# Half-block products in the output product of two feed-forward layers

## The chip, the cores and the metric

The kernel runs on one core of a Trainium2 chip. The metric is the time of one execution on the device, in microseconds. Before the change it is 1256.23 us, the median of three runs (1256.0 to 1259.08). The profile is of one more execution, which took 1256.96 us.

## The reference

Two decoder layers work on 512 positions of width 1024: a convolution module with a feed-forward layer behind it, then attention with a second feed-forward layer. Each part normalises its input and is added to the residual x. The change lies in the feed-forward layers, and there in the second product:

```python
def swiglu_ffn(h, w_in, w_out):
    gate, up = jnp.split(h @ w_in, 2, axis=-1)
    return (jax.nn.silu(gate) * up) @ w_out

def reference(...):
    for i in range(DEPTH):                      # DEPTH = 2
        ...
        x = x + y.astype(x.dtype)
        h = rmsnorm(x, norm_ffn[i])
        x = x + swiglu_ffn(h, ffn_w_in[i], ffn_w_out[i]).astype(x.dtype)
```

The inner width is 2816, that is 22 rows of 128. All arrays are 32-bit floats.

## The kernel before

Everything is held transposed: x is eight tiles `x[m]` of 128 features by 512 positions, and the inner activations are 22 tiles `y` of 128 by 512. TensorE multiplies in a reduced format, so each operand is split into a high part (a copy into the format, ScalarE) and a low part (the rest, a subtraction on VectorE), and each product is made of three matmuls: high by high, high by low, low by high (`mm3`, lines 257 to 260).

Weights come as units of up to 1024 columns in a fixed list (lines 124 to 162). `w_dma` (line 183) loads a unit from SyncE's queue into one of three raw buffers, `w_hi` (line 191, copy in line 198) and `w_lo` (line 201, subtraction in line 207) split it into one of two buffers for the high and one of two for the low part. `next_w` (line 210) takes the next unit and has three more loaded ahead.

`ffn` (line 705) makes one feed-forward layer in three stages. First the five rows f = 0 to 4 of gate and up are made in the plain way. Then `pair` (line 867) makes the other 17 rows. It is already a scheme of seven products of half blocks instead of eight: `product` (line 834, matmul in line 840) multiplies blocks of 128 by 128 weights with 256 positions; sums of weights are made by accumulating transfers from GpSimd's queue (`s_acc`, issue in line 807) and by additions on GpSimd (lines 814 and 815), and split in `s_part` (lines 823 and 824). Last comes the output stage (lines 932 to 991): for each of the eight output tiles m the 22 rows are summed in one bank of PSUM, 66 matmuls of 512 columns (lines 258 to 260, named `st<-ah,wh` and so on), the weights in units of 8, 8 and 6 rows per m in the order `OUT_ORDER`. The operands are `ah[f]` and `al[f]`, the parts of `y[f]`, split by `divide` (lines 738 to 742). The sum in PSUM is added to `x[m]` (line 985 in layer 0, 990 in layer 1). In layer 0, `finish_x` (line 304) then makes the next layer's operand parts hh and hl and adds the square of `x[m]` to `acc` on GpSimd (lines 292, 293, 300, 302); in layer 1 `x[m]` goes out to memory (line 991), the last tile in two pieces of 256 columns. `rope_tables` (line 995) makes two tables for the attention; it is called once within layer 0's output stage.

The order on each engine comes from a scheduler, except for instructions that go through `tc.keep_in_program_order`; these keep the order in which they are written. `held` does so while `hold[0]` is set, which before the change ends after the first 16 rows of m = 0 and 1 (line 972).

Of the kernel before, what the change touches and what calls it, by code (L numbers as in the profile page):

```python
# [19 lines left out]
P = 128  # L20
T = 512
# [70 lines left out]
OUT_ORDER = [(m, b) for b in range(3) for m in range(2)] + [(m, b) for m in range(2, NK) for b in range(3)]  # L92
OUT_N = 256
# [15 lines left out]
def trunk(ctx: ExitStack, tc: tile.TileContext, A, out):  # L109
# [27 lines left out]

    def add_ffn(l):
# [5 lines left out]
        for m, b in OUT_ORDER:  # L144
            add("fw_o8", l * 16 + m * 2 + b, 1024) if b < 2 else add("fw_o6", l * 8 + m, 768)
# [37 lines left out]
    def w_dma(i):  # L183
        if i in raws or i >= len(units):
            return
        ap, cols = units[i]
        t = wp.tile([P, 1024], F32, tag="wr", name=f"wr{i}")
        raw_dma[i] = after(nc.sync.dma_start(t[:, :cols], ap), state.get("behind"))
        raws[i] = t
# [98 lines left out]
    def split_x(m, gcol):  # L288
# [3 lines left out]
        nc.scalar.activation(hh[m], x[m], AF.Copy, scale=g)  # L292
        nc.vector.scalar_tensor_tensor(hl[m], x[m], g, hh[m], ALU.mult, ALU.subtract)

    def sum_x(m, acc, eng=None, on_v=False):
# [3 lines left out]
        else:  # L299
            nc.scalar.activation(sq, x[m], AF.Square)  # L300
        if m > 0:
            (eng or nc.gpsimd).tensor_tensor(acc, acc, sq, ALU.add)  # L302
# [402 lines left out]
    def ffn(acc, gnext, layer, between=None):  # L705
# [9 lines left out]
        with ExitStack() as cx:  # L715
# [216 lines left out]
            pss, w, ws = {0: bank()}, {0: next_w(False)}, {}  # L932

            def out_mm(m, fs):
                wh, wl = w[m]
                for f in fs:
                    c = slice(f % 8 * P, (f % 8 + 1) * P)
                    mm3(pss[m], wh[:, c], wl[:, c], ah[f], al[f], f == 0, f == NF - 1)

            def parts(*fs):  # L940
                for f in fs:
                    divide(f, fo)

            hold[0] = True
            out_mm(0, range(4))
            w_hi(state["next"])
            w_lo()
# [4 lines left out]
            parts(4, 5, 6, 7)  # L952
            pss[1] = bank()
            w[1] = next_w(False)
            out_mm(1, range(4))
            out_mm(0, range(4, 8))
            parts(8, 9, 10, 11)
            w_hi(state["next"])
            w_lo()
            out_mm(1, range(4, 8))  # L960
            parts(12, 13, 14, 15)
            w[0] = next_w(False)
            w_hi(state["next"])
            out_mm(0, range(8, 16))
            w_lo()
            parts(16, 17, 18)
            w[1] = next_w(False)
            w_hi(state["next"])
            out_mm(1, range(8, 16))
            w_lo()  # L970
            parts(19, 20, 21)
            hold[0] = False
            acc = new_acc() if gnext is not None else None
            for m, b in OUT_ORDER[4:]:
                if m not in pss:
                    pss[m] = bank()
                ps = pss[m]
                w[m] = next_w()
                if (m, b) == (3, 0) and layer == 0:
                    between()  # L980
                out_mm(m, range(8 * b, min(8 * b + 8, NF)))
                if b < 2:
                    continue
                if gnext is not None:
                    nc.vector.tensor_tensor(x[m], x[m], ps, ALU.add)
                    finish_x(m, gnext, acc, fin(m))
                else:
                    n = OUT_N if m == NK - 1 else T
                    for c in range(0, T, n):
# [844 lines left out]
```

## Time and profile before

| what | value |
|---|---|
| median of three runs | 1256.23 us |
| profiled execution, its time | 1256.96 us |
| profiled execution, its span in the trace | 1255.2 us |
| TensorE busy | 1226.4 us, 98% |
| VectorE, ScalarE, GpSimd busy | 827.4, 566.0, 340.8 us |
| output stage of layer 0, first to last matmul's start | 422.69 to 547.57 us |
| output stage of layer 1 | 1125.85 to 1250.73 us |
| memory read in the span | 146.73 MB |

PE is TensorE's matmuls and PEld its weight loads, DVE is VectorE, ACT ScalarE, POOL GpSimd, SP SyncE. A row of the time line has the start, the duration, the engine, the line in the kernel, the operation, its output and inputs, and in brackets the idle time in front with the engine that ended it. A row of groups has the count behind the x, then busy time and mean duration in ns, then the idle time in front. Matmuls overlap in their ends, so the pace of TensorE is read from the time between two starts, and not from a matmul's duration. A row of stretches has the busy time of each engine with its count, then TensorE's granted clock (1.00 is full), the share of time in which the DMA engines worked, and GB/s. Some matmul records can be missing.

### The profile page before, as it was taken

The page shows a single profiled execution, that of the slowest core. Times are in us where ns is not written, and L with a number is a line of the kernel's source. Part 1 is how long each engine was busy: PE and PEld are TensorE (multiplying, and loading weights), DVE is VectorE, ACT ScalarE, POOL GpSimd, SP SyncE. Part 2 cuts the span into 40 slices and gives each one's busy share as a digit, 9 for nine tenths or more (in the row PEclk, how much of TensorE's full clock was granted, in tenths as well). Part 3 has the DMA queues.
Part 4 walks back from the last instruction along what each step waited for, and adds up shares of the span by engine and source line. Part 5 has one row for each costly group of instructions (what it writes and reads, how often), then busy time and mean ns, then how long its engine had stood idle before and what let it go on. Part 6 is the DMA issues. An engine that isn't in the chain of part 4 may idle for free.

```text
span 1255.2 us, 20744 instructions
## 1 busy us (share of the span) xinstructions
PE 1226.4 (98%) x8015; PEld 1036.0 (83%) x8015; DVE 827.4 (66%) x1455; ACT 566.0 (45%) x1046; POOL 340.8 (27%) x395
## 2 busy tenths in 40 slices
PE   9999899999999999999998999999999999999998
PEld 6787788799999988887777776667878999998886
DVE  6995587788888735336697777753497766656221
ACT  5221464445554533223453677773354555544111
POOL 2010021144444001132332465651303444410000
PEclk9999999999999999999998999999999999999999
DMA  8757636457766233253166011001624877722331
GB/s 304 267 133 270 170 101 185 118 148 180 185 177 161 60 110 99 93 151 112 60 150 162 18 25 36 1 18 52 197 88 112 205 192 188 181 82 97 110 112 43
DMA packets 82115, 161.62 MB, mean 129 GB/s; under 512 B 36064, under 2 KB 36960, under 8 KB 80480
## 3 DMA queue, kind: packets, MB, share of 16 engines
q1 hardware_dynamic: 65808, 108.54, 28.3%
q0 software_dynamic: 16208, 51.75, 16.2%
q8 instruction: 63, 1.03, 0.3%
q14 instruction: 36, 0.29, 0.1%
HBM read 146.73 MB, written 5.28 MB: 121 GB/s over the span
## 4 chain that ended last, share of the span: by engine, by line
PE 72%; DVE 9%; issue 9%; POOL 5%; ACT 3%; DMA 1%; SPq 1%; DVEq 0%; POOLq 0%; ACTq 0%
PE st L840 17%; PE pp L258 7%; PE pp L260 7%; PE pp L259 7%; PE st L260 7%; PE st L258 7%; PE st L259 7%; PE O L1576 3%; PE cpe L496 2%; POOL S L815 1%; POOL S L814 1%; PE T L1550 1%; DVE Pm L1522 1%; PE S L1519 1%; POOL S L807 1%
## 5 line engine op out<-in xcount | busy, mean ns | idle before, releaser
L198 ACT ACTIVATE wh<-wr 128x1024 fp32r<-128x1024 f32 (+3 forms) x158 | 160.4, 1015 | 299.1 <-PE st L259 143.3
L207 DVE TENSOR_TENSOR wl<-wr,wh 128x1024 fp32r<-128x1024 f32 (+3 forms) x158 | 191.0, 1209 | 123.6 <-ACT wh L198 123.2
L840 PE MATMUL st<-bh,sh 128*128 128x256 f32 x680 | 194.1, 285 | 0.7 <-DVE t L865 0.7
L840 PE MATMUL st<-bh,sl 128*128 128x256 f32 x680 | 192.5, 283 | 1.1 <-DVE sl L824 1.1
L840 PE MATMUL st<-bl,sh 128*128 128x256 f32 x680 | 192.0, 282 | 0.0
L258 PE MATMUL pp<-hh,wh 128*128 128x512 f32 x400 | 158.8, 399 | 2.6 <-ACT wh L198 2.4
L260 PE MATMUL pp<-hh,wl 128*128 128x512 f32 x400 | 157.4, 396 | 1.7 <-DVE wl L207 1.7
L259 PE MATMUL pp<-hl,wh 128*128 128x512 f32 x400 | 157.9, 396 | 0.0
L824 DVE TENSOR_TENSOR sl<-S,sh 128x512 fp32r<-128x512 f32 x136 | 117.4, 899 | 46.9 <-ACT sh L823 45.4
L260 PE MATMUL st<-ah,wl 128*128 128x512 f32 x352 | 139.6, 396 | 0.0
L258 PE MATMUL st<-ah,wh 128*128 128x512 f32 x352 | 139.5, 396 | 0.0
L259 PE MATMUL st<-al,wh 128*128 128x512 f32 x352 | 139.5, 396 | 0.0
L840 PEld LDWEIGHTS st<-bh,sh 128*128 128x128 f32 x680 | 129.9, 191 | 2.5 <-DVE t L865 1.1
L840 PEld LDWEIGHTS st<-bh,sl 128*128 128x128 f32 x680 | 130.1, 191 | 1.5 <-DVE sl L824 1.5
L840 PEld LDWEIGHTS st<-bl,sh 128*128 128x128 f32 x680 | 130.5, 192 | 0.1
L1537 POOL TENSOR_SCALAR Pm<-Pm,sm,gates 128x512 f32<-128x512 f32 (+3 forms) x128 | 79.8, 636 | 64.9 <-DVE sm L1533 52.2
L258 PEld LDWEIGHTS pp<-hh,wh 128*128 128x128 f32 x400 | 75.3, 188 | 23.9 <-ACT wh L198 5.0
L302 POOL TENSOR_TENSOR acc<-acc,sq 128x512 f32<-128x512 f32 x18 | 30.9, 1718 | 226.8 <-ACT sq L300 208.9
L260 PEld LDWEIGHTS pp<-hh,wl 128*128 128x128 f32 x400 | 75.2, 188 | 20.4 <-DVE wl L207 3.3
L814 POOL TENSOR_TENSOR S<-S,wr 128x512 f32<-128x512 f32 x34 | 53.9, 1586 | 135.1 <-DMA wr<-fw_in 72.9
L259 PEld LDWEIGHTS pp<-hl,wh 128*128 128x128 f32 x400 | 75.4, 188 | 18.2 <-issue 1.1
L1523 ACT ACTIVATE Pm<-Pm,mx 128x512 f32<-128x512 f32 (+3 forms) x128 | 71.0, 557 | 37.7 <-DVE mx L1522 33.2
(292 smaller groups left out, 2556.1 us busy)
## 6 DMA issues: line engine op xcount, KB each, us to landing
S<-fw_x POOLq DMA_DIRECT2D x68, 512.0 KB, 6.0
wr<-fw_in SPq DMA_DIRECT2D x46, 512.0 KB
wr<-fw_o SPq DMA_DIRECT2D x32, 512.0 KB
bd<-bands POOLq DMA_DIRECT2D x12, 1280.0 KB, 12.3
r<-fw_x SPq DMA_DIRECT2D x34, 256.0 KB
wr<-cw_in SPq DMA_DIRECT2D x14, 512.0 KB
wr<-fw_o SPq DMA_DIRECT2D x16, 384.0 KB
wr<-fw_s SPq DMA_DIRECT2D x8, 512.0 KB
```

The source lines that it names most:

```text
L198: parted(after(nc.scalar.activation(hi[:, :cols], raws[i][:, :cols], AF.Copy), pin.get(AF)))
L207: parted(after(nc.vector.tensor_tensor(lo[:, :cols], raws[i][:, :cols], hi[:, :cols], ALU.subtract), pin.get(ALU)))
L258: held(nc.tensor.matmul(ps, wh, xh, start=first, stop=False))
L259: held(nc.tensor.matmul(ps, wh, xl, start=False, stop=False))
L260: held(nc.tensor.matmul(ps, wl, xh, start=False, stop=last))
L302: (eng or nc.gpsimd).tensor_tensor(acc, acc, sq, ALU.add)
L814: pe(nc.gpsimd.tensor_tensor(t[:, :T], S[n][:, :T], w[:, :T], ALU.add))
L824: pe(nc.vector.tensor_tensor(l_[:, c], z, h_[:, c], ALU.subtract))
L840: pe(nc.tensor.matmul(ps[:, :H], p_[:, k], m_[c][:, t], start=first and c == 0 and q == 0, stop=last and c == 3 and q == 2, skip_group_che ...
L1523: at_[AF] = nc.scalar.activation(Pt, Pt, AF.Exp, bias=mx, scale=-1.0, accum_out=sm)
L1537: nc.gpsimd.tensor_scalar(Pt, Pt, sm[:, k:k + 1], gates[:, t + k, br * 16 + h:br * 16 + h + 1], ALU.mult, ALU.mult)
L1576: pe(nc.tensor.matmul(o[par * 64:par * 64 + 64, P * kc:], vf[br][:, kc, g], Us[par][kc], start=False, stop=last))
```

## The change

The 22 rows of the output product are now used in three groups. Rows 0 to 3 (`EARLY`) come first, for all eight m: "plain" pieces of four rows, two m to a unit of 1024 columns, added to x by `keep_plain`. Rows 4 to 7 (`LATE`) are eight more pieces of four rows, one for each m with a unit of 512 columns, put between other work as `LATE_AT` says (a slot named "Q"). The 14 rows 8 to 21 form a block product of two by two halves: 7 rows by 7 rows, output tiles 0 to 3 and 4 to 7, positions 0 to 255 and 256 to 511. It is made of seven products instead of eight, in the order 1, 4, 2, 3, 5, 6, 7.

Each product has a half block of weights of 4 x 7 x 128 = 3584 columns, in units of 1024, 1024, 1024 and 512. For products 1, 4 and 7 this is a quarter of the weights itself, loaded as before. For 2, 3, 5 and 6 it is a sum of quarters: a plain load from SyncE's queue (`s_base`) and accumulating loads from GpSimd's queue (`s_more`), split by `split_sum` into the same two buffers. The operands are halves of the tiles y (`direct`) or differences and sums of them (`z_1`, `z_4`, `z_on`, on GpSimd, then `summed`). Output sums are partly kept in PSUM, and after each product each of its four tiles of 256 columns is added to or taken from x (`out_add`). One slot of the loop splits the weights of the next slot, issues the slot's matmuls, then the steps that `todo` has for the slot, then the sums into x.

All of the stage is now kept in the written order, `finish_x` too. The steps of `rope_tables` are spread over the slots of layer 0, and its load of the positions moves from GpSimd's queue to SyncE's. Tiles x[0] to x[3] are finished in product 5, x[4] to x[7] in product 7.

```diff
+LATE = 4
+NO = (NF - EARLY - LATE) // 2
+QCOLS = 4 * NO * P
+QU = (QCOLS + 1023) // 1024
+OUT_SEQ = (1, 4, 2, 3, 5, 6, 7)
+OUT_RAW = {1: 0, 4: 1, 7: 3}
+OUT_SUMS = ((2, 3, (2,)), (3, 3, (2, 0)), (5, 3, (2, 0, 1)), (6, 0, (2,)))
+OUT_NEW = tuple(z[0] for z in OUT_SUMS)
+LATE_AT = {(1, 1): (0,), (4, 0): (1,), (4, 2): (4,), (2, 0): (2,), (2, 2): (5,), (3, 0): (3,), (3, 2): (6,),
+           (5, 1): (7,)}
...
-        nc.scalar.activation(hh[m], x[m], AF.Copy, scale=g)
-        nc.vector.scalar_tensor_tensor(hl[m], x[m], g, hh[m], ALU.mult, ALU.subtract)
+        parted(nc.scalar.activation(hh[m], x[m], AF.Copy, scale=g))
+        parted(nc.vector.scalar_tensor_tensor(hl[m], x[m], g, hh[m], ALU.mult, ALU.subtract))
...
+            def z_new(name, g, a, b):
+                z = zs[name, g] = fo.tile([P, len(PAIRS[g]) * H], F32, tag=f"{name}{g}", name=nm("z"))
+                for k, i in enumerate(PAIRS[g]):
+                    pe(nc.gpsimd.tensor_tensor(z[:, k * H:(k + 1) * H], half(*a(i)), half(*b(i)), ALU.subtract))
...
+            def s_base(k, u):
+                p, q_, _ = OUT_SUMS[k]
+                n = "S6" if p == 6 else "S"
+                sums[n, u] = fo.tile([P, ucols(u)], F32, tag=f"{n}{u}", name=nm("So"))
+                pe(nc.sync.dma_start(sums[n, u], quarter(layer, q_, u)[0]))
+
+            def s_more(k, u):
+                p, _, qs = OUT_SUMS[k]
+                pe(nc.gpsimd.dma_start(sums["S6" if p == 6 else "S", u], quarter(layer, qs[-1], u)[0], accum_op=ALU.add))
+
+            def split_sum(p, u):
+                n = ucols(u)
+                z = sums["S6" if p == 6 else "S", u]
+                hi = wp.tile([P, 1024], F32R, tag="wh", name=nm("soh"), bufs=2)
+                lo = wp.tile([P, 1024], F32R, tag="wl", name=nm("sol"), bufs=2)
+                pe(nc.scalar.activation(hi[:, :n], z, AF.Copy))
+                pe(nc.vector.tensor_tensor(lo[:, :n], z, hi[:, :n], ALU.subtract))
+                return hi, lo
...
+            def products(p, u, w):
+                wh, wl = w
+                done = []
+                for k in range(ucols(u) // P):
+                    j, i = divmod(8 * u + k, NO)
+                    ps = target(p, j)
+                    h_, l_ = opnd[p, i // 2]
+                    t = slice(i % 2 * H, (i % 2 + 1) * H)
+                    c = slice(k * P, (k + 1) * P)
+                    for r, (a, b) in enumerate(((wh, h_), (wh, l_), (wl, h_))):
+                        pe(nc.tensor.matmul(ps, a[:, c], b[:, t], start=p in (1, 4) and i == 0 and r == 0,
+                                            stop=i == NO - 1 and r == 2, skip_group_check=True))
+                    if i == NO - 1:
+                        done.append(j)
+                return done
+
+            ADDS = {1: (0, 0, -1), 4: (0, 0, 1), 2: (4, 1, -1), 3: (0, 1, -1), 5: (0, 1, 1), 6: (4, 1, 1), 7: (4, 0, 1)}
...
+            def out_add(p, j):
+                dm, t, sign = ADDS[p]
+                m = j + dm
+                xs = x[m][:, t * H:(t + 1) * H]
+                pe(nc.vector.tensor_tensor(xs, xs, target(p, j), ALU.add if sign > 0 else ALU.subtract))
...
+                elif p in (5, 7):
+                    finals.append(m)
...
+            for g in range(NG):
+                at(("P", (0, 1, 1, 2, 2)[g]), L(direct, 1, g, "oA", 0, 0, -1.0))
+                at(("P", (1, 1, 1, 2, 2)[g]), L(z_1, g))
+                at((1, (0, 0, 1, 1, 2)[g]), L(z_4, g))
+                e = (0, 0, 1, 2, 3)[g]
+                at((1, e), L(direct, 4, g, "oB", 1, 0))
+                at((4, e), L(summed, 2, g, "oA", "zz"))
+                at((4, e + 1), L(z_on, g, 1, ALU.add))
+                at((2, e), L(summed, 3, g, "oB", "zz"))
+                at((3, e), L(direct, 5, g, "oA", 1, 1))
+                at((5, (0, 1, 2, 3, 4)[g]), L(z_on, g, 0, ALU.subtract))
+                at((5, e), L(summed, 6, g, "oB", "zw"))
+                at((6, e), L(summed, 7, g, "oA", "zz"))
+            for f in range(EARLY, EARLY + LATE):
+                at(("P", 3), L(divide, f, fo))
+            for u in range(QU):
+                at(("P", 1 + u // 2), L(s_base, 0, u))
+                at(("P", 2 + u // 2), L(s_more, 0, u))
+                at((2, u), L(s_more, 1, u))
+                at((3, u), L(s_more, 2, u))
+                at((1, u), L(s_base, 3, u))
+                at((4, u), L(s_more, 3, u))
...
+            for n, (p, u) in enumerate(slots):
+                w = ready if p in OUT_NEW else next_w(False)
+                if n + 1 < len(slots):
+                    p1, u1 = slots[n + 1]
+                    if p1 in OUT_NEW:
+                        ready = split_sum(p1, u1)
+                    else:
+                        split_next()
+                elif state["next"] < state["end"]:
+                    split_next()
+                if p == "Q":
+                    late(u, w)
...
+                else:
+                    done = products(p, u, w)
+                for f in todo.pop((p, u), ()):
+                    f()
...
+                for j in done:
+                    out_add(p, j)
+                while finals:
+                    m = finals.pop(0)
+                    finish_x(m, gnext, acc, fin(m))
```

More of the change, by code (lines that the diff above doesn't have):

```diff
@@ L143, in add_ffn @@
             add("fw_in", l * n + i, 1024)
-        for m, b in OUT_ORDER:
-            add("fw_o8", l * 16 + m * 2 + b, 1024) if b < 2 else add("fw_o6", l * 8 + m, 768)
+        for i in range(4):
+            add("fw_p", l * 4 + i, 1024)
+        for z in OUT_SEQ:
+            for u in range(QU):
+                if z in OUT_RAW:
+                    units.append(quarter(l, OUT_RAW[z], u))
+                for m in LATE_AT.get((z, u), ()):
+                    add("fw_r", l * NK + m, LATE * P)
     add_ffn(0)
@@ L965, in ffn @@
[L965 to L971, printed above, removed]
-            hold[0] = False
[L973 to L989, printed above, removed]
-                        nc.vector.tensor_tensor(x[m][:, c:c + n], x[m][:, c:c + n], ps[:, c:c + n], ALU.add)
-                        nc.sync.dma_start(out[m][:, c:c + n], x[m][:, c:c + n])
@@ new lines, in z_1, with z_4, z_on @@
+            def z_1(g):
+                z_new("zz", g, lambda i: (0, i, 0), lambda i: (0, i, 1))
+            def z_4(g):
+                z_new("zw", g, lambda i: (0, i, 1), lambda i: (1, i, 1))
+            def z_on(g, t, op):
+                z = zs["zz", g]
+                for k, i in enumerate(PAIRS[g]):
+                    c = slice(k * H, (k + 1) * H)
+                    ab = (z[:, c], half(1, i, t)) if op == ALU.add else (half(1, i, t), z[:, c])
+                    pe(nc.gpsimd.tensor_tensor(z[:, c], *ab, op))
@@ new lines, in split_sum, with target @@
+            def split_sum(p, u):
[6 more added lines that the diff above has]
+                return hi, lo
+            AD, B = {}, {}
+            def target(p, j):
+                if p == 1 and j not in AD:
+                    AD[j] = bank()
+                if p == 4 and j not in B:
+                    B[j] = bank()
+                return B[j][:, :H] if p == 4 else AD[j][:, H:] if p in (2, 5) else AD[j][:, :H]
@@ new lines, in ffn @@
+            slots = [("P", n) for n in range(1, 4)]
+            for p in OUT_SEQ:
+                for u in range(QU):
+                    slots.append((p, u))
+                    slots.extend(("Q", m) for m in LATE_AT.get((p, u), ()))
+            for n, f in enumerate(tables):
+                at(slots[1 + n], f)
+            acc = new_acc() if gnext is not None else None
+            plain(1)
+            keep_plain(0)
+            for f in todo.pop(("P", 0)):
+                f()
+            keep_plain(1)
@@ L996, in rope_tables @@
+            assert not todo, todo
+            hold[0] = False
+        return acc
+    rope = []
+    def rope_tables(fo):
         rp = hx[0].enter_context(tc.tile_pool(name="rp", bufs=1))
@@ L1673, in trunk @@
     cx0.close()
-    rope = []
-    acc = ffn(acc, V_NM1, 0, lambda: rope.extend(rope_tables()))
+    acc = ffn(acc, V_NM1, 0, rope_tables)
     cosT, sinT = rope
```

157 lines of the change are left out of this document (104 added, 53 removed).

## The prediction

> **What bounds the kernel now.** I read the page first, then the stretches of the two feed-forward layers, then single rows around their ends.
>
> ```profile
> span 1255.2 us, 20744 instructions
> PE 1226.4 (98%) x8015; PEld 1036.0 (83%) x8015; DVE 827.4 (66%) x1455; ACT 566.0 (45%) x1046; POOL 340.8 (27%) x395
> PE 72%; DVE 9%; issue 9%; POOL 5%; ACT 3%; DMA 1%; SPq 1%; DVEq 0%; POOLq 0%; ACTq 0%
> ```
>
> TensorE is busy 98% of the span and makes most of the chain: work taken off TensorE is time, if nothing else becomes late. The next two answers give stretches with TensorE alone (busy, count, clock, DMA share, GB/s), then with all engines: the paired products and the output stage of layer 0, then of layer 1.
>
> ```profile
> 430.00:545.00 115.00, 115.00 (x493) 1.00 0.31 95
> 1131.00:1250.00 119.00, 119.00 (x509) 1.00 0.28 92
> 960.00:1125.00 165.00, 165.00 (x1386) 1.00 0.65 168
> 258.00:426.00 168.00, 167.29 (x1373) 165.00 (x1373) 135.24 (x180) 85.54 (x162) 68.31 (x59) 1.00 0.64 165
> 426.00:549.00 123.00, 123.00 (x532) 99.09 (x531) 54.27 (x71) 41.53 (x57) 16.52 (x18) 1.00 0.31 96
> 1130.00:1252.00 122.00, 121.13 (x519) 97.08 (x517) 41.90 (x51) 29.46 (x37) 0.00 (x0) 1.00 0.27 90
> ```
>
> The output stage has no gap on TensorE, full clock, and VectorE at 54 of 123 us in layer 0 and 42 of 122 in layer 1. A matmul of 512 columns goes in 119/509 = 0.234 us, one of 256 columns in 165/1386 = 0.119: half the columns cost half the time, so nothing is lost by halving.
>
> **Products.** Per layer, 14 rows cost 14 x 8 x 3 = 336 matmuls of 512 columns, 336 x 0.234 = 78.6 us. In their place stand 7 products of 4 x 7 blocks x 3 = 588 matmuls of 256 columns, 588 x 0.119 = 70.0. The other 8 rows (192 matmuls) stay. That is -8.6 a layer, **-17.2** in all, and the most that can be had.
>
> **Each product ends in a short unit.** A half block has 3584 columns of weights, so its units are 1024, 1024, 1024 and 512 columns. The two buffers of the split weights stay: ScalarE may split unit n+1 only when TensorE has left unit n-1, and VectorE's low part comes after it. The rows are the end of layer 0's stage and the weight split behind it, one group of 12 narrow matmuls, and one restart after a wait.
>
> ```profile
> 547.33 0.39 PE L259 MATMUL st<-al,wh 128*128 128x512 f32 x1
> 547.57 0.39 PE L260 MATMUL st<-ah,wl 128*128 128x512 f32 x1
> 547.76 1.06 ACT L198 ACTIVATE wh<-wr 128x1024 fp32r<-128x1024 f32 x1 [3.15 <-PE st L259]
> 548.00 0.69 DVE L985 TENSOR_TENSOR x<-x,st 128x512 f32<-128x512 f32 x1 [2.13 <-PE st L260]
> 548.73 0.71 ACT L292 ACTIVATE hh<-x,vec 128x512 fp32r<-128x512 f32 x1
> 548.86 1.23 DVE L207 TENSOR_TENSOR wl<-wr,wh 128x1024 fp32r<-128x1024 f32 x1 [0.17 <-ACT wh L198]
> 549.35 0.62 ACT L300 ACTIVATE sq<-x 128x512 f32<-128x512 f32 x1
> 425.65 1.43 PE st L840 x12
> 958.61 0.39 PE L840 MATMUL st<-bh,sl 128*128 128x256 f32 x1 [0.53 <-DVE sl L824]
> ```
>
> ScalarE starts 0.04 after the last reader of the old high part has ended (547.33 + 0.39 = 547.72), which with narrow matmuls is about 0.1 after TensorE turns to the short unit. Then 1.06, 0.04 and 1.23 pass and 0.05 to TensorE: 2.5 us. The short unit gives 1.43 (12 matmuls), and the first two matmuls of the next unit need no low part, 0.24 more. So TensorE waits 0.8 and restarts slower by 0.1 (0.39 where others have 0.28): 0.85 at each end of a product. No late piece stands behind a short unit (they stand behind the first three units). Six ends a layer lie before another product, and layer 0's last before the attention's first weights: 13 x 0.85 = **+11.1**. Bounds: 0 if the split were ready early, 1.5 if VectorE is behind as well. The full units last 24 x 0.119 = 2.86, against the same 2.5: no wait, but only 0.4 to spare.
>
> **Work moved onto VectorE and GpSimd.** Grouped rows of layer 0's output stage, one narrow piece, then four rows in which the two engines meet.
>
> ```profile
> L207 DVE TENSOR_TENSOR wl<-wr,wh 128x1024 fp32r<-128x1024 f32 (+1 forms) x24 | 27.3, 1136 | 50.1 <-ACT wh L198 50.1
> L742 DVE TENSOR_TENSOR al<-y,ah 128x512 fp32r<-128x512 f32 x18 | 11.2, 685 | 0.0
> L302 POOL TENSOR_TENSOR acc<-acc,sq 128x512 f32<-128x512 f32 x6 | 10.9, 1816 | 114.5 <-ACT sq L300 100.8 <-DVE wl L207 13.7
> 304.94 0.42 DVE L858 TENSOR_TENSOR y<-t,g 128x256 f32<-128x256 f32 x1
> 305.03 1.18 POOL L807 DMA_DIRECT2D S<-fw_x  x1 [4.71 <-DMA S<-fw_x]
> 305.27 2.83 DVE L824 TENSOR_TENSOR sl<-r,sh 128x512 fp32r<-128x512 f32 x1
> 305.77 1.77 POOL L814 TENSOR_TENSOR S<-S,wr 128x512 f32<-128x512 f32 x1
> 307.61 1.64 POOL L815 TENSOR_TENSOR S<-S,wr 128x512 f32<-128x512 f32 x1
> ```
>
> Split columns grow from 22,528 to 33,280 a layer (12.9 us more at 1.23 per 1024). Operand pieces: 18 of 0.69 (12.4) become 4 of 0.69, 21 narrow ones of 0.42 and four sums of 3 x 0.69 + 0.42 (21.6). Sums into x: 8 of 0.69 (5.5) become 28 of 0.42 and 16 of 0.69 (22.8). VectorE gets 39 us more: 93 in layer 0, 81 in layer 1, where TensorE needs about 117. On the mean it fits, as it did in the paired stage (135 of 168). It costs where VectorE's written order meets a short unit.
>
> GpSimd adds 28 differences of 256 columns a layer. The trace has none of that width: half of one of 512 (1.30, the least of L814's, quoted below) is 0.65, the whole is 1.30; I take 0.7. What they block counts more: the subtraction at 305.27, beside GpSimd's work, took 2.83 instead of 0.69. [...]
>
> *Entry to the products.* The last plain slot (24 x 0.234 = 5.6) and the first unit (2.86) give VectorE 8.5 us. It owes two splits (2.46), four pieces of rows 4 to 7 (2.76) and two sums (1.38), which stand ahead of the second split and wait for TensorE: 6.6, in layer 0 a rope step more. GpSimd, not bound to slots, runs up to five differences in between (3.5). 10.1 - 8.5 = 1.6 late; without GpSimd nothing. I take 1.5 a layer, **+3.0**.
>
> *Finishing x in layer 0.* Products 5 and 7 finish x four times each, and the instructions now keep the written order: sum into x 0.42, hh 0.71, square 0.62, only then the next high split 1.06 and low split 1.23, with 0.3 of handovers 4.3 us after a block's last matmul. The unit between gives 2.86 + 0.24 and what is left of the unit behind that block (0.36, 0.71, 1.07, 0 in the four units). The late piece in product 5 covers its first. Beyond the 0.85 counted already this makes 0.5, 0.7 and 1.2 in product 5, 0.9 and 0.7 in product 7: 4.0. VectorE also owes there hl, operand pieces, and turns lost to GpSimd's differences and squares; those are 1 to 4 us more. I take **+6.0** (between 4 and 9). Before, 15 us of matmuls lay between two finished tiles, so this cost nothing.
>
> **Hidden, and what hides it.** The sums of weights: 6 half-block loads of 1.83 MB a layer, 16 of them as accumulating transfers of at most 512 KB; traffic rises from 11.5 to 20.7 MB, 172 GB/s over 120 us, near the 165 of the paired stage.
>
> ```profile
> S<-fw_x POOLq DMA_DIRECT2D x68, 512.0 KB, 6.0
> 996.41 1.19 POOL L807 DMA_DIRECT2D S<-fw_x  x1 [3.79 <-DMA S<-fw_x]
> 996.96 1.29 DVE L824 TENSOR_TENSOR sl<-S,sh 128x512 fp32r<-128x512 f32 x2 [0.66 <-ACT sh L823]
> 998.34 1.30 POOL L814 TENSOR_TENSOR S<-S,wr 128x512 f32<-128x512 f32 x1 [0.74 <-DVE sl L824]
> 550.66 0.69 DVE L302 TENSOR_TENSOR acc<-acc,sq 128x512 f32<-128x512 f32 x1
> 556.32 0.79 PE ssq L318 x8
> 1251.17 0.75 DVE L990 TENSOR_TENSOR x<-x,st 128x256 f32<-128x256 f32 x2 [8.24 <-PE st L260]
> 1251.61 0.82 SPq L991 DMA_DIRECT2D outT<-x  x2
> ```
>
> 6.0 us to landing, against 10 to 14 between an accumulation and the split that reads it (three units, a short one, late pieces): hidden. The first accumulations wait on GpSimd's queue for their plain loads; behind them stand differences that product 4 alone needs, 15 us on. Rope: 14 steps, one a slot, in VectorE's order, and the positions' load moves from GpSimd's queue to SyncE's, ahead of weight loads that are fetched three units early; they stood in slack and still mostly do. Attention's sum of squares runs 8 us after the stage's end, and acc was ready at 551.35; VectorE may now be 5 us behind at that point, so 0 to 2. The kernel's end keeps its last narrow sum and output transfer: 0, at best -0.4.
>
> **Sum.** -17.2 + 11.1 + 3.0 + 6.0 = +2.9 on the profiled execution's 1256.96, which stands 0.7 above the median of 1256.23: **1260.0** profiled, 1259 on the median. I name 1260.0, since the open ends (attention's start, rope) only add. About 0.3%, 3.8 us, is what a measurement can tell from no change.
>
> **Rivals.**
>
> *Faster, 1248.* The queues cover more than I allow: half of the waits at the products' ends (5.5), 1.0 at the entries, 2.0 at the finishing: -17.2 + 8.5 = -8.7. For: in the paired stage TensorE was busy 167.3 of 168 us with VectorE at 135. Against: there a pair leaves 10 us for a split, here the short unit leaves 1.43.
>
> *Clearly slower, 1272: GpSimd holds VectorE off the splits.* At 305.27 the subtraction lost 2.1 us to an accumulation's issue and the addition right behind it; at 996.96, with no addition queued, two of them took 1.29 beside an issue, no loss. The changed queue has about seven such places a layer (differences behind accumulations in the last plain slots and in product 4), 14 x 2.1 = 29 us, of which late pieces, each with about 1.5 to spare, cover over half: +12 on 1260. It decides once the differences are ready when the issue before them ends. Against: most of them wait for VectorE's reads first. [...]
>
> *Landing too late, 1266.* If accumulating transfers take over 10 us, TensorE waits at the first units of products 2, 3, 5 and 6, some 0.8 each in both layers. Against: 6.0 at the same traffic.
>
> **Chances.** Forecast 0.45 (its own range 1254 to 1265), faster 0.22, GpSimd 0.25, landing 0.08. Faster by over 0.3%: 0.20 from the first rival. Within: 0.27 from the forecast and 0.06 from the edges of the rivals, 0.33. Slower: 0.18 of the forecast, 0.23 and 0.06: 0.47. The range, 1247 to 1273, holds all but the outer halves of two rivals.
>
> **What would show it.** TensorE's matmuls of the stage summing to about 117 us a layer; waits of 0.8 to 0.9 on the low part at each first unit behind a short one; none or few inside products 2 and 3; layer 0's stage about 130 us and layer 1's about 123 (now 125 each). Wrong, if layer 1 gains under 1 us or over 5, if the waits name DMA, or if the gaps lie inside product 4.

## The result, and the profile after

The changed kernel takes 1274.25 us, the median of four runs (1270.59 to 1276.03), where the kernel before took 1256.12 in four runs beside it (1255.34 to 1259.08). The ratio is 1.0136, with a 95% interval of 1.0106 to 1.0167: slower. The forecast was 1260.0, the range ended at 1273.

The profiled execution took 1270.59 us with a span of 1268.7, against 1256.96 and 1255.2 before. So 13.6 us are to be explained here, and the forecast had put 2.9 there. The other three runs are 2 to 5.4 us longer still; their mean granted clock was 0.991, the profiled one's 0.996. The page of the profile after:

```profile
span 1268.7 us, 22185 instructions
PE 1211.6 (95%) x8519; PEld 1047.5 (83%) x8519; DVE 916.5 (72%) x1604; ACT 603.0 (48%) x1124; POOL 413.9 (33%) x482
PE 63%; DVE 12%; issue 10%; POOL 6%; ACT 4%; DMA 2%; SPq 2%; POOLq 0%; DVEq 0%; ACTq 0%
```

TensorE works 14.8 us less (1226.4 to 1211.6) and the span is 13.5 us longer: the saving is there, and TensorE waits 28 us more. Its share of the chain fell from 72 to 63%; VectorE's and GpSimd's rose. The two output stages, as stretches with all engines (TensorE, its loads, VectorE, ScalarE, GpSimd, then clock, DMA share, GB/s):

```profile
417.60:551.20 133.60, 120.57 (x794) 108.91 (x792) 99.97 (x146) 59.99 (x97) 45.20 (x49) 0.99 0.62 151
1135.90:1265.30 129.40, 118.99 (x794) 108.72 (x792) 88.56 (x127) 50.53 (x80) 33.41 (x40) 0.99 0.64 160
```

They lasted 125.0 us each, without a gap. Now layer 0's lasts 133.6 (+8.6) and layer 1's 129.4 (+4.4): 13.0 of the 13.6. The rest nearly cancels out: up to the paired products of layer 0 -1.9, these (248.0 to 417.6, before 249.9 to 422.7) -3.2, from there to the paired products of layer 1 +0.1, these (959.9 to 1135.9, before 956.3 to 1125.8) +6.4, the end -0.9. The paired products are code that the change doesn't touch.

Where TensorE waits in layer 1, from its time line (from start to start it is 0.28 more than the idle time in the brackets, and that is about what is lost: 0.65 idle are 0.93 from start to start, where 0.12 is the pace, and the matmul behind comes another 0.10 late):

```profile
1166.39 0.38 PE L1063 MATMUL st<-oz,wl 128*128 128x256 f32 x1 [3.41 <-DVE wl L226]
1177.19 0.38 PE L1063 MATMUL st<-oz,wl 128*128 128x256 f32 x1 [0.65 <-DVE wl L226]
1193.49 0.38 PE L1063 MATMUL st<-oz,sol 128*128 128x256 f32 x1 [0.54 <-DVE sol L1041]
1209.79 0.38 PE L1063 MATMUL st<-oz,sol 128*128 128x256 f32 x1 [0.54 <-DVE sol L1041]
1229.55 0.58 PE L1063 MATMUL st<-oz,sol 128*128 128x256 f32 x1 [3.99 <-DVE sol L1041]
1244.68 0.38 PE L1063 MATMUL st<-oz,sol 128*128 128x256 f32 x1 [0.65 <-DVE sol L1041]
1255.54 0.39 PE L1063 MATMUL st<-oz,wl 128*128 128x256 f32 x1 [0.63 <-DVE wl L226]
```

Five of the seven are the first low part behind a short unit, 0.81 to 0.93 lost each. The first row is another thing: the second unit of product 1, 3.69 lost. So is the fifth, the first unit of product 5: 4.27. All wait for VectorE's low part. This is what VectorE (DVE) and GpSimd (POOL) did ahead of these two:

```profile
1155.20 1.22 DVE L226 TENSOR_TENSOR wl<-wr,wh 128x1024 fp32r<-128x1024 f32 x1 [0.17 <-ACT wh L217]
1156.35 7.66 DVE L761 TENSOR_TENSOR al<-y,ah 128x512 fp32r<-128x512 f32 x4
1155.01 1.73 POOL L1033 DMA_DIRECT2D So<-fw_q  x2 [9.41 <-DMA So<-fw_q]
1156.23 5.41 POOL L1007 TENSOR_TENSOR z<-y,y 128x256 f32<-128x256 f32 x7
1222.69 0.86 POOL L1033 DMA_DIRECT2D So<-fw_q  x1 [3.93 <-DVE sol L1041]
1223.25 5.15 POOL L1020 TENSOR_TENSOR z<-y,z 128x256 f32<-128x256 f32 x7
1224.81 4.68 DVE L1041 TENSOR_TENSOR sol<-So,soh 128x1024 fp32r<-128x1024 f32 x1 [0.17 <-ACT soh L1040]
1229.41 0.41 DVE L1076 TENSOR_TENSOR x<-x,st 128x256 f32<-128x256 f32 x1
```

At 1156.23 GpSimd begins seven differences, one behind the other, until 1161.64. VectorE's four small subtractions, 0.69 each when alone, take 7.66 beside them. At 1223.25 seven more run until 1228.40; the subtraction that starts at 1224.81, 1.22 when alone, ends at 1229.49, 1.1 after the last of them. It was held through five differences and got in between none of them. TensorE, which needed it, starts at 1229.55. The differences at 1156.23 are those of `z_4` for product 6's operands, listed in the first slots of product 1; those at 1223.25 are for product 7's (`z_on`, listed in the slots of product 5). Their data had long been there; GpSimd, which no slot holds, ran each seven as soon as the accumulating transfer ahead of them was issued.

In layer 0 the same two places show (at product 5's start with a run of four differences), and behind them the finishing of x:

```profile
448.29 0.58 PE L1063 MATMUL st<-oz,wl 128*128 128x256 f32 x1 [3.57 <-DVE wl L226]
510.80 0.38 PE L1063 MATMUL st<-oz,sol 128*128 128x256 f32 x1 [1.94 <-DVE sol L1041]
521.06 0.40 PE L1063 MATMUL st<-oz,sol 128*128 128x256 f32 x1 [1.04 <-DVE sol L1041]
527.30 0.39 PE L1063 MATMUL st<-oz,sol 128*128 128x256 f32 x1 [1.09 <-DVE sol L1041]
531.49 0.39 PE L1063 MATMUL st<-oz,sol 128*128 128x256 f32 x1 [1.10 <-DVE sol L1041]
552.46 0.50 PE L277 MATMUL pp<-hh,wh 128*128 128x512 f32 x1 [1.10 <-ACT wh L217]
```

Behind the long wait in layer 1 TensorE goes at half clock. Stretches of TensorE alone (busy, count, clock, DMA share, GB/s):

```profile
1220.00:1225.00 5.00, 5.00 (x33) 1.00 0.97 223
1226.00:1229.00 3.00, 0.00 (x0) 1.00 0.12 21
1229.60:1232.80 3.20, 3.20 (x15) 0.50 0.00 0
1233.00:1240.00 7.00, 7.00 (x50) 1.00 0.44 148
```

15 matmuls in 3.2 us are 0.21 each, the pace before and behind is 0.12, which would be 1.8: with the slow restart some 1.5 us more are lost. In layer 0 the same stands behind the wait in product 1 (a granted clock of 0.50 from 448.3 to 451.1, 13 matmuls in 2.8 us), 1.3 us.

### The profile page after: what moved, and what is told of

Its sections match the earlier page's. It is cut to its first block, busy times and chain, and to the rows that moved or that the text cites. A ratio compares the mean times of both kernels' runs of the same rounds, so it can differ in the third digit from the quotient of the medians.

```text
span 1268.7 us, 22185 instructions
## 1 busy us (share of the span) xinstructions
PE 1211.6 (95%) x8519; PEld 1047.5 (83%) x8519; DVE 916.5 (72%) x1604; ACT 603.0 (48%) x1124; POOL 413.9 (33%) x482
## 4 chain that ended last, share of the span: by engine, by line
PE 63%; DVE 12%; issue 10%; POOL 6%; ACT 4%; DMA 2%; SPq 2%; POOLq 0%; DVEq 0%; ACTq 0%
PE st L859 15%; PE st L1063 8%; PE pp L279 6%; PE pp L277 6%; PE pp L278 6%; PE O L1759 3%; PE cpe L515 2%; DVE wl L226 2%; POOL S L834 2%; PE pv L1594 2%; POOL S L833 2%; PE T L1733 1%; DVE sol L1041 1%; POOL S L826 1%; PE S L1702 1%
## 5 line engine op out<-in xcount | busy, mean ns | idle before, releaser
L217 ACT ACTIVATE wh<-wr 128x1024 fp32r<-128x1024 f32 (+3 forms) x158 | 154.2, 976 | 223.4 <-PE pp L278 60.8
L226 DVE TENSOR_TENSOR wl<-wr,wh 128x1024 fp32r<-128x1024 f32 (+3 forms) x158 | 186.6, 1181 | 32.0 <-ACT wh L217 31.4
L843 DVE TENSOR_TENSOR sl<-S,sh 128x512 fp32r<-128x512 f32 x136 | 111.8, 859 | 55.2 <-ACT sh L842 54.2
L842 ACT ACTIVATE sh<-S 128x512 fp32r<-128x512 f32 x136 | 79.2, 620 | 21.6 <-POOL S L833 21.5
L826 POOL DMA_DIRECT2D S<-fw_x x34 | 40.3, 1186 | 145.0 <-DMA S<-fw_x 143.9
L1063 PE MATMUL st<-oz,soh 128*128 128x256 f32 x448 | 81.8, 284 | 0.5 <-ACT soh L1040 0.5
L1705 DVE CUSTOM_DVE_ANT_0 Pm<-S,mask 128x512 f32<-128x512 f32 (+3 forms) x128 | 59.2, 484 | 28.2 <-PE S L1703 27.6
## 6 DMA issues: line engine op xcount, KB each, us to landing
bd<-bands POOLq DMA_DIRECT2D x12, 1280.0 KB, 12.8
```

Of the source, the lines that this page charges most:

```text
L217: parted(after(nc.scalar.activation(hi[:, :cols], raws[i][:, :cols], AF.Copy), pin.get(AF)))
L226: parted(after(nc.vector.tensor_tensor(lo[:, :cols], raws[i][:, :cols], hi[:, :cols], ALU.subtract), pin.get(ALU)))
L842: pe(nc.scalar.activation(h_[:, c], z, AF.Copy))
L843: pe(nc.vector.tensor_tensor(l_[:, c], z, h_[:, c], ALU.subtract))
L1063: pe(nc.tensor.matmul(ps, a[:, c], b[:, t], start=p in (1, 4) and i == 0 and r == 0, stop=i == NO - 1 and r == 2, skip_group_check=True))
```

## The experiments

**Theory.** GpSimd's differences, queued back to back, hold a subtraction of VectorE through the whole run and not for one turn, at two places a layer: in the last plain slots and at product 5's start. **Rivals:** VectorE is simply overbooked there (its own work, the late pieces, the finishing); or the short units cost more than they seem; or landing transfers. Each time stands against the kernel before on the same chip: its medians were 1254.57 for the first four kernels, 1253.3 for the next four and 1253.26 for the last four.

**a1_nodiff: without the differences.** The operands of products 2, 3, 6 and 7 come from one constant tile, GpSimd makes no differences; all else is done.

```diff
-                z = zs[name, g]
+                z = flat[:, :len(PAIRS[g]) * H]
...
-                at(("P", (1, 1, 1, 2, 2)[g]), L(z_1, g))
-                at((1, (0, 0, 1, 1, 2)[g]), L(z_4, g))
-                at((4, e + 1), L(z_on, g, 1, ALU.add))
-                at((5, (0, 1, 2, 3, 4)[g]), L(z_on, g, 0, ALU.subtract))
```

> Leaves out the 28 GpSimd differences of a layer (the operands of products 2, 3, 6 and 7 are made from a constant tile instead, with the same copies and subtractions). In the changed kernel's profile TensorE waits 3.9 us (layer 0) and 3.7 (layer 1) ahead of the second unit of product 1, and 2.2 and 4.3 ahead of product 5; a run of six or seven GpSimd differences covers each. Theory A (a run of differences holds one VectorE subtraction to its end): the waits at product 1 fall under 0.5, those at product 5 to the 0.9 of a short unit; layer 0's stage 133.6 -> 128, layer 1's 129.4 -> 122.5; about -12 us in all. Theory B (VectorE simply has too much in its written order there): each wait stays within 1 us of what it was. Theory C (sums of weights land late): the wait at product 5 stays, the one at product 1 too.

Measured: 1261.66 us, ratio 1.0057 (1.004 to 1.0075); stages of 130.0 and 123.2 us, 3.6 and 6.2 less than in the changed kernel. Both long waits are gone: product 5 starts after 0.82 lost in both layers, an ordinary end of a product. In their place smaller waits appear inside product 4 in both layers, the largest 1.38 and 1.32, on ScalarE's copy of weights; what held the copy isn't settled. The differences' load is the cause; whether it is their work or the place where they run, this kernel can't say.

**a2_paced: the same differences at other places.** `z_4` goes to product 2's slots and the subtractions of `z_on` to product 3's, one group a slot, each behind an accumulating transfer, which itself waits for VectorE's subtraction.

```diff
-                at((1, (0, 0, 1, 1, 2)[g]), L(z_4, g))
+                at((2, g), L(z_4, g))
...
-                at((5, (0, 1, 2, 3, 4)[g]), L(z_on, g, 0, ALU.subtract))
+                at((3, g), L(z_on, g, 0, ALU.subtract))
```

> The same differences, but those for product 6 are written in the slots of product 2 and those for product 7 in the slots of product 3, between the accumulating loads, whose wait on VectorE's split keeps GpSimd to the pace of the slots. Theory A: no run longer than two differences meets a split; the wait at product 1 under 1 us, at product 5 about 0.9; layer 0's stage -5, layer 1's -6; about -11 in all. Theory B: no change within 2 us. Theory C: no change, or slower, since the loads are issued later.

Measured: 1260.03 us, ratio 1.0041 (1.0022 to 1.006); 130.0 and 122.0 us. With all differences made, the stages are as short as without any, so it is the place and the run's length, not the work. New waits of up to 1.42 in products 2 and 3, beside the runs of two, cost 3.0 of the gain in layer 0 and 1.3 in layer 1. GpSimd and VectorE in product 3 of layer 1:

```profile
1208.77 0.87 POOL L1033 DMA_DIRECT2D So<-fw_q  x1 [3.06 <-DVE sol L1041]
1209.38 1.73 POOL L1020 TENSOR_TENSOR z<-y,z 128x256 f32<-128x256 f32 x2
1209.68 2.52 DVE L1041 TENSOR_TENSOR sol<-So,soh 128x1024 fp32r<-128x1024 f32 x1 [0.17 <-ACT soh L1040]
1218.84 1.22 DVE L1041 TENSOR_TENSOR sol<-So,soh 128x1024 fp32r<-128x1024 f32 x1 [0.17 <-ACT soh L1040]
```

A run of two differences makes the subtraction 2.52 instead of 1.22: it ends 1.09 after the second (1209.38 + 1.73 = 1211.11), as the one in the changed kernel ended 1.1 after the seventh. Here, too, the delay is what was left of the run.

**a3_late: the late pieces behind short units.** The eight plain pieces are put where the forecast's waits are. In layer 1 one half of x[5] leaves for memory before its late piece has been added.

```diff
-LATE_AT = {(1, 1): (0,), (4, 0): (1,), (4, 2): (4,), (2, 0): (2,), (2, 2): (5,), (3, 0): (3,), (3, 2): (6,),
+LATE_AT = {(1, 3): (0,), (4, 3): (1,), (2, 3): (2,), (3, 3): (3,), (5, 3): (4,), (6, 3): (5,), (4, 1): (6,),
            (5, 1): (7,)}
```

> Six of the eight late pieces stand behind the short units of products 1, 4, 2, 3, 5 and 6 instead of behind full units. Theory of the short unit (2.5 us of split against 1.43 of matmuls): six waits of 0.8 to 0.9 a layer go, -5 a layer, -10 in all; the waits behind GpSimd's differences stay or grow. Rival (VectorE's load): what the late pieces covered before comes back in other slots, the total moves by under 3 us.

Measured: 1267.45 us, ratio 1.0097 (1.0077 to 1.0118); stages of 133.6 and 129.4, to a tenth those of the changed kernel. The waits behind the short units went, and others came: 1.99 and 2.17 in layer 0; 2.06 with 1.03 at product 4's first unit and 3.36 ahead of product 5 in layer 1; the mean granted clock of the profiled execution was 0.987, against 0.996. The pieces also covered the units beside which they stood; moved, they move the wait. That the stages agree to a tenth is chance: product 1 lost 2.6 and 1.9 less than in the changed kernel, as a4_finish will show.

**a4_finish: finishing x one slot later.** `finish_x` now stands behind the next slot's split, not ahead of it.

```diff
                     split_next()
+                while finals:
+                    m = finals.pop(0)
+                    finish_x(m, gnext, acc, fin(m))
...
-                while finals:
-                    m = finals.pop(0)
-                    finish_x(m, gnext, acc, fin(m))
+            while finals:
+                m = finals.pop(0)
+                finish_x(m, gnext, acc, fin(m))
```

> In layer 0 the finishing of x (hh, hl, square, sum) is written one slot later, behind the next split instead of ahead of it. Theory of the written order: the 6.4 us that products 5 to 7 wait beyond their short units falls to about 2, -4 us in layer 0, nothing in layer 1. Rival (ScalarE and VectorE have too much there whatever the order): under 1.5 us.

Measured: 1264.64 us, ratio 1.0086 (1.0055 to 1.0117); layer 0's stage 129.2, 4.4 less, and the attention's first matmul follows without a gap. Only in part is the 4.4 the finishing's: behind product 5's start its waits fell by 4.2, but some 3.1 were lost again, with a lower granted clock behind two waits (0.50 from 509.1 to 511.5, 0.74 on the mean from 531.9 to 534.2), and the entry to the products, where no instruction is changed, lost 1.8 instead of 5.2 us. Layer 1's, in which nothing is finished and no instruction is changed, was 131.1, with the same two waits (4.01 and 4.26); the mean granted clock of the profiled execution was 0.991, against 0.996. ScalarE's time line in the changed kernel, then in this one:

```profile
523.45 0.72 ACT L311 ACTIVATE hh<-x,vec 128x512 fp32r<-128x512 f32 x1 [3.16 <-DVE x L1076]
524.08 0.62 ACT L319 ACTIVATE sq<-x 128x512 f32<-128x512 f32 x1
524.60 1.04 ACT L1040 ACTIVATE soh<-So 128x1024 fp32r<-128x1024 f32 x1
```

```profile
521.85 1.07 ACT L1040 ACTIVATE soh<-So 128x1024 fp32r<-128x1024 f32 x1 [1.95 <-PE st L1063]
522.83 0.73 ACT L311 ACTIVATE hh<-x,vec 128x512 fp32r<-128x512 f32 x1
```

In the changed kernel the copy that TensorE needs stands behind hh and the square, 1.15 us of work, which themselves waited 3.16 for x. Here it stands ahead of them and waits only for TensorE.

The entry of layer 0 shows something else. VectorE's pieces and the seven differences, which are the same as in the changed kernel, take turns here. They do so at the entry in both layers of a3_late and in layer 1 of d1_even (below), too, from which these rows are, GpSimd, then VectorE:

```profile
1150.99 7.92 POOL L1007 TENSOR_TENSOR z<-y,y 128x256 f32<-128x256 f32 x7
1151.34 4.71 DVE L761 TENSOR_TENSOR al<-y,ah 128x512 fp32r<-128x512 f32 x4
```

The seven differences take 7.92 instead of 5.41, the four pieces 4.71 instead of 7.66, and product 1 loses 0.9 to 2.5 us in these four cases, where it lost 3.7 and 5.2 (half clock included) in the changed kernel. So a run of differences can hold VectorE to its end, and doesn't always; which of the two comes isn't explained by any run here. At product 5's start the hold showed in all of these kernels (TensorE's wait in layer 1: 3.36 in a3_late, 4.26 in a4_finish, 3.52 idle in d1_even).

**b1_memset: a write between the differences.** Each difference is followed by a GpSimd write of eight columns, which reads nothing.

```diff
                     pe(nc.gpsimd.tensor_tensor(z[:, k * H:(k + 1) * H], half(*a(i)), half(*b(i)), ALU.subtract))
+                    pe(nc.gpsimd.memset(turn, 0.0))
```

(and the same behind line 1020)

> After each GpSimd difference of the changed kernel stands a GpSimd write of 8 columns, which reads nothing; the number and place of the differences stay. Theory A says that VectorE's waiting subtraction gets in only when GpSimd stops reading: with a write between two differences it is held for one difference at most (some 0.7 us), so the waits at product 1 fall from 3.7-3.9 to 1.5-2 and at product 5 from 2.2 and 4.3 to about 1-1.5; stages of about 131 and 124. If GpSimd keeps what it holds from one instruction to the next whatever stands between, or if the sheer time of the differences counts, the waits stay at 3.5 and more.

Measured, one run: 1277.17 us, stages of 135.1 and 131.2. Both waits are still there: 4.32 and 2.35 in layer 0, 2.53 with 1.89 and then 4.52 in layer 1. GpSimd, then VectorE, at product 5 of layer 1:

```profile
1228.34 1.06 POOL L1022 TENSOR_TENSOR z<-y,z 128x256 f32<-128x256 f32 x1
1229.02 0.43 POOL L1023 MEMSET turn<- 128x8 f32 x1
1229.08 1.05 POOL L1022 TENSOR_TENSOR z<-y,z 128x256 f32<-128x256 f32 x1
...
1233.41 0.37 POOL L1023 MEMSET turn<- 128x8 f32 x1
1229.91 4.93 DVE L1044 TENSOR_TENSOR sol<-So,soh 128x1024 fp32r<-128x1024 f32 x1 [0.17 <-ACT soh L1043]
```

The next difference starts 0.06 after the write did, and the subtraction again waits until the last is over. A write in between opened no turn.

**b2_vec: the differences on VectorE.**

```diff
-                    pe(nc.gpsimd.tensor_tensor(z[:, k * H:(k + 1) * H], half(*a(i)), half(*b(i)), ALU.subtract))
+                    pe(nc.vector.tensor_tensor(z[:, k * H:(k + 1) * H], half(*a(i)), half(*b(i)), ALU.subtract))
...
-                    pe(nc.gpsimd.tensor_tensor(z[:, c], *ab, op))
+                    pe(nc.vector.tensor_tensor(z[:, c], *ab, op))
```

> The 28 differences of a layer run on VectorE, in the same slots, instead of on GpSimd: 28 x 0.35 = 10 us more for VectorE, none for GpSimd. Theory A: the waits of 3.7-3.9 and 4.3 go, others of up to 1.5 come in the slots that hold four differences; stages 129 to 131 in layer 0 and 121 to 124 in layer 1, -6 to -10 in all. Theory B (VectorE's load): clearly slower than the changed kernel, +5 and more.

Measured: 1263.7 us, ratio 1.0095 (1.0072 to 1.0117); 134.6 and 123.8. In layer 1 the long waits went and 5.6 us with them, though VectorE has the work itself now. In layer 0, where it also has the rope steps and the finishing, 18 waits of up to 1.4 took the place of the changed kernel's 13 and its long ones. So overbooking of VectorE isn't what costs layer 1, and is close in layer 0.

**c2_pf: paced and finished later** (the edits of a2_paced and a4_finish together).

> Differences paced as in the run before and x finished one slot later. If the two gains are separate they add: layer 0's stage 130.0 - 4.4 = 125.6, the attention starts without a wait (-1.3), layer 1's stays at 122. Total about 1254 to 1256. Rival (both gains are of the same waits): layer 0 no better than 129.

Measured: 1252.35 us, ratio 0.9985 (0.9966 to 1.0003); 126.2 and 122.0. Layer 0's stage is 7.4 shorter than in the changed kernel, and 3.8 shorter than in a2_paced, which differs from it by the finishing alone: that is the finishing's worth, on top of the pacing's 3.6. The interval holds 1: no difference from before can be told.

**c1_all: that, and five late pieces behind short units.**

```diff
+LATE_AT = {(1, 3): (0,), (4, 3): (1,), (2, 3): (2,), (3, 3): (3,), (5, 3): (4,), (2, 1): (5,), (4, 1): (6,),
            (5, 1): (7,)}
```

> Paced, finished later, and five of the late pieces behind the short units of products 1, 4, 2, 3 and 5, the other three behind the second units of products 4, 2 and 5. Theory of the short unit, now without long GpSimd runs: five waits of 0.85 a layer go: layer 0 about 121.5, layer 1 about 118, near the 117 of the matmuls alone; total about 1246. Rival (VectorE's written order leaves no room where late pieces were taken away): stages within 1.5 us of those of the run without the move.

Measured: 1258.46 us, ratio 1.0046 (1.0031 to 1.0061); 127.1 and 125.7, worse than c2_pf by 0.9 and 3.7. In layer 1 the largest wait is now at product 4's first unit, 2.40 and 1.04. ScalarE and TensorE there:

```profile
1163.66 1.06 ACT L217 ACTIVATE wh<-wr 128x1024 fp32r<-128x1024 f32 x1 [4.80 <-DMA wr<-fw_q]
1164.77 0.50 PE L1063 MATMUL st<-oz,wh 128*128 128x256 f32 x2 [2.25 <-ACT wh L217]
```

ScalarE waited 4.80 for the weights themselves: with VectorE out of the way, the transfers are next. At product 4 of a3_late it waited for weights, too (3.03 and 4.47).

**d1_even: no short unit.** The changed kernel with four equal units of 896 columns.

```diff
-QU = (QCOLS + 1023) // 1024
+UW = NO * P
+QU = QCOLS // UW
```

(`ucols`, `quarter` and the loop of `products` use UW in place of 1024)

> The changed kernel with one size changed: a half block's 3584 columns go in four units of 896 columns instead of 1024, 1024, 1024 and 512, so that no unit is short. A unit is 21 matmuls, 2.5 us, against 0.1 + 0.93 + 0.04 + 1.08 + 0.05 = 2.2 us for its split. Theory of the short unit: the waits of 0.8 to 0.9 at the ends of products 1, 4, 2 and 6 go (four to five a layer), the waits behind long GpSimd runs stay: -3 to -4 in each layer, -7 in all. Rival (the wait belongs to the change of product, whose operands or sums are late): it stays, total within 2 us of the changed kernel.

Measured: 1261.37 us, ratio 1.0067 (1.0045 to 1.0089); 132.7 and 123.7. In layer 1 the waits of 0.8 to 0.9 at the first units of products 2, 3, 6 and 7 are gone, 3.4 us. Product 4's first unit waits 0.98 and 0.90 for the copy of weights that land late, as in c1_all. The entry lost 2.8 less there, where the engines took turns as shown above; in layer 0, where VectorE was held, it lost as much as in the changed kernel, in two waits of 1.61 and 2.47. Layer 0 as a whole gained 0.9, where 3 to 4 were expected: the waits at products 2 and 3 went, and those of the finishing grew. The wait at product 5 stays (layer 1):

```profile
1221.02 0.38 PE L1063 MATMUL st<-oz,sol 128*128 128x256 f32 x1 [3.52 <-DVE sol L1041]
```

The short units and the runs of differences are separate costs.

**d2_even_pf: no short unit, paced, finished later** (the edits of d1_even and c2_pf).

> Even units, differences paced, x finished one slot later. Theory: three separate waits, so the gains add. From the run without even units (stages 126.2 and 122.0) six ends of 0.85 go: 121 and 117 to 118; total about 1243. Rival (transfers of weights become the next limit, as one wait on them showed in product 4 when six late pieces were moved): gain under 4 us, with ScalarE's split waiting for a transfer.

Measured: 1244.37 us, ratio 0.9926 (0.9903 to 0.9949): faster than the kernel before. 122.2 and 118.9 us.

**d3_spread: the operand pieces, too, one group a slot.**

```diff
-                e = (0, 0, 1, 2, 3)[g]
+                e = g
...
-                at((4, e + 1), L(z_on, g, 1, ALU.add))
+                at((4, min(e + 1, 3)), L(z_on, g, 1, ALU.add))
```

> As the run with all three edits, and the operand pieces of a product one a slot instead of two, one, one, none. VectorE then has 1.0 + 0.6 + 0.35 us in each slot of 2.5 instead of 2.7 in the first. If VectorE's order is what is left: another -1 to -3. If transfers are what is left: no change.

Measured: 1245.57 us, ratio 0.9941 (0.9921 to 0.996); 123.6 and 120.6, 1.4 and 1.7 longer than in d2_even_pf: no gain.

**d4_s6: product 6's sums loaded later.** On top of d3_spread, the loads of product 6's sum leave products 1 and 4 for products 2 and 3.

```diff
-                at((1, u), L(s_base, 3, u))
-                at((4, u), L(s_more, 3, u))
+                at((2, u), L(s_base, 3, u))
+                at((3, u), L(s_more, 3, u))
```

> As the run before, and the loads for the sum of product 6 issued in products 2 and 3, which load no other weights, instead of 1 and 4, which load plain units too. If transfers bind in products 1 and 4: a wait of 1 to 2.5 us there goes in each layer, -2 to -5 in all. If not: no change, or slower by the accumulations that now share products 2 and 3.

Measured: 1242.93 us, ratio 0.9923 (0.99 to 0.9946), the least of all. The stages:

```profile
418.00:539.20 121.20, 117.55 (x794) 107.28 (x793) 104.15 (x146) 60.69 (x97) 44.27 (x45) 1.00 0.66 169
1117.80:1235.80 118.00, 116.49 (x793) 106.75 (x792) 92.12 (x127) 50.55 (x80) 33.83 (x40) 1.00 0.68 175
```

121.2 and 118.0 against 125.0 each before and 123.6 and 120.6 in d3_spread, 2.4 and 2.6 less. About 1.0 of each is the wait at product 4's last unit (0.76 and 0.62 idle in d3_spread), which is gone. In layer 1 ScalarE had waited 3.04 there for weights to land; in layer 0 a split had taken 2.25 beside differences. The rest came off in products 2 and 3, so the traffic is shown as the cause for that one wait alone. The largest waits left are 1.44 and 1.24 in layer 0 and 1.12 in layer 1. By the whole time it can't be told from d2_even_pf (the intervals overlap nearly wholly); both beat the two kernels.

## Why the prediction was wrong

The sum was made for the profiled execution, and there it can be compared term by term (both layers, us):

| step | forecast | measured | from |
|---|---|---|---|
| matmuls | -17.2 | -18.9 | stages less their waits: 133.6 - 18.0 and 129.4 - 13.9, against 125.0 each |
| ends of products | +11.1, with the thirteenth | +10.4 | 12 in the stages by 0.87, the mean of nine that stand alone (0.80 to 0.93) |
| entry to the products | +3.0 | +8.8 | 3.85 and 1.3 at half clock; 3.69 |
| product 5's start | not in the sum | +6.2 | 2.22 and 4.27, less an end of 0.87 each, and 1.5 at half clock |
| finishing x | +6.0 | +6.3 | waits in products 5 to 7 of layer 0, less the ends |
| sum of the stages | +2.9 | +13.0 | 8.6 and 4.4; the rows give 12.8 |
| attention's start, the thirteenth end in it | 0 to 2, beside that end | about 2.7 | idle 1.10 and 1.28 before its first matmuls |

**The step that failed** is the entry to the products: "GpSimd, not bound to slots, runs up to five differences in between (3.5)", and from it "I take 1.5 a layer". Two things stand against it. Seven differences ran there in one go, all of `z_4`, and held VectorE for about 5 us a layer: four pieces took 7.66, where 2.76 was counted. With 7 x 0.74 = 5.2 in place of 3.5 the sentence's own sum gives 6.6 + 5.2 - 8.5 = 3.3, and 3.69 and 3.85 were measured; so the blocking was seen and the length of the run was not, nor the half clock behind the wait (1.3). That each difference takes its whole time from VectorE, as 6.6 + 3.5 has it, is shown by no run as a rule: beside seven of them the four pieces lost 4.9 here and 1.95 at the entry of d1_even. And GpSimd ran ahead at a second place, too, that the sum put at nothing, product 5's start: 6.2 us, because the subtraction was held through the rest of the run and not for one difference. The two make 12.0, more than the 10.1 by which the sum fell short; the matmuls gave 1.7 more than counted, and the other rows nearly cancel out. a1_nodiff takes both waits away by leaving the differences out, a2_paced by moving them. d1_even, without short units, keeps the wait at product 5 in both layers and the entry's in layer 0.

The rival "GpSimd holds VectorE off the splits" had the mechanism, "accumulation's issue and the addition right behind it", and its time of 1272 is 1.4 above the profiled one. Its working was not right: it counted seven places a layer of 2.1 each, mostly covered, where there are two of 2.2 to 4.3, and it named product 4 where the run stands ahead of product 5. The reason given against it, that most differences "wait for VectorE's reads first", fails at both places, where seven (four in layer 0's second) run without a wait. That its time came out so near is luck.

**What held.** Half the columns cost half the time: the matmuls even saved 0.8 a layer more than counted, since a narrow one goes in 0.118 and not in 0.119 (a wide one in 0.234). The end of a product: 0.85 worked out, 0.80 to 0.93 measured, and gone with equal units at products 2 and 3 (d1_even). The finishing: 6.0 and 6.3, in the places named, products 5 and 7, though product 5's last one came out late in product 6 (1.38 at its second unit); its five terms leave out one of 0.5 at product 7's last unit, where 0.80 was lost. Finishing one slot later takes back 3.8 (c2_pf against a2_paced) and the attention's wait. One difference took 5.15 / 7 = 0.74, where 0.7 was taken. The landing of accumulating transfers is hidden, as the page's DMA part has them:

```profile
So<-fw_q POOLq DMA_DIRECT2D x24, 512.0 KB, 5.9
```

and no wait of TensorE in the two stages names a transfer. Of the tests that the forecast set, the stages of about 130 and 123 failed it with 133.6 and 129.4: layer 1 was to gain between 1 and 5 on its 125.0, and lost 4.4. The faster rival, half of the waits at the ends hidden, is refuted: none was, short of removing the short units.

**What the range missed.** The median stands 3.7 above the profiled execution. A mean clock of 0.991 instead of 0.996 is 0.005 x 1270 = 6.4 us at most, about the 5.5 by which two of those runs are longer; so more stretches at half clock fit the difference. That was worked out, not tried. Nor was what makes the paired products vary: 169.6 and 176.0 in the two layers of the changed kernel, 172.8 and 169.6 before, 169.6 to 173.4 in the experiments. The trace shows where layer 1's 6.4 lie: TensorE sat idle 3.5 us in three waits on `t`, VectorE's difference of two products (line 884), and was busy for 171.84 us, where the same stage took 168.97 before. Ahead of the longest, at 1076.69, GpSimd had waited 8.07 us for a transfer to land, and its additions, ScalarE's copy and VectorE's work followed late. Before the change layer 0 had two such waits. The stage holds the same instructions in all kernels, so its 6.4 in layer 1 and -3.2 in layer 0 are not put down to the change, nor cleared of it.

## What to carry to other kernels

GpSimd, which no slot of the written order held, ran its independent steps as soon as their data were there, all in one run (seven in 5.15 us). Price such a run by its whole length at the worst place that it can reach, even if the other engine sometimes gets its turns, and pace it by putting each step behind something that waits, as the accumulating transfers do in a2_paced. A pipeline of two buffers is as tight as its smallest unit: 512 columns gave 1.43 us against 2.5 for a split, with equal units of 896 most of these waits were gone. When a saving of 19 us turns into a loss, look for separate waits and take them away one by one: here three edits, none of which alone reached the kernel before (1.0041, 1.0086, 1.0067), together turned 1.0136 into 0.9926.

## What the runs showed of the hardware

- At product 5's start a VectorE subtraction of 128x1024, 1.22 us when alone, that met a run of GpSimd differences ended about 1.1 us after the last of them, with seven of them (4.68 us in the changed kernel) and with writes in between (4.93 in b1_memset), and so did one beside a run of two in a2_paced (2.52). In none of these rows did it get its turn at the end of one difference. At the entry VectorE did get it in four cases on record: four subtractions took 4.71 beside seven differences (d1_even, layer 1) and not 7.66, and the differences came about 1.15 apart and not 0.70. No run shows what decides. In the paired products, where the second of two additions needs the first one's result, VectorE did get in between them: the subtraction at 305.27 before the change took 2.83 and ended at 308.10, while the second addition was running (307.61 to 309.25).
- Behind a wait of 4.27 us TensorE went at a granted clock of 0.50 for 3.2 us (1229.6 to 1232.8). The wait of 3.85 in layer 0 was followed by half clock, too (0.50 from 448.3 to 451.1), and that of 3.69 in layer 1 was not (1.00 from 1166.4 to 1170). But a shorter one was followed by it as well: one of 2.22 in a4_finish (0.50 from 509.1 to 511.5), where the same wait of 2.22 in the changed kernel was not (1.00 from 511 to 514). No run shows what decides here either.
